# A bias table's trip through memory moved behind the first weight loads, and block sums built by one addition instead of sixteen

## The chip, the core and the metric

One core of one Trainium2 chip runs the whole program. The metric is the device time in microseconds of one execution, as the median over runs. TensorE does the matmuls, VectorE (DVE), ScalarE (ACT) and GpSimd (POOL) the element work, and SyncE (SP) issues the loads and stores on one queue, in order.

## What is computed

A sequence of 256 tokens of width 1024 goes through two blocks. The first block is a pool mixer beside an 8-head causal attention with a relative-position bias, then a gated MLP with a short convolution (width 2816) and a gated embedding. The second block has two layers: a native sparse attention (NSA) and a mixture of experts (MoE), then a latent attention (MLA) and again an MoE. Each MoE has 16 experts, of which two are chosen for a token. All arithmetic is float32.

Cut to what the change touches, the reference is

```python
# first block: bias of the attention logits, by bucket of the distance
bias_own = rel_bias.T[:, rel_bucket(t[:, None] - key_pos)]       # 8 heads
l_own = (q @ k.T) * scale + bias_own

# second block, NSA, compressed branch (for k and for v)
blk = t[:, tok_idx] + pe[None, None, :, None, :]   # 15 windows of 32 tokens, stride 16
blk = blk.transpose(0, 1, 3, 2, 4).reshape(B, 15, 4, 32 * 64)
k_cmp = silu(blk @ w1) @ w2
```

## The kernel before, in words

The weights don't fit on the chip; they are streamed from memory once, in chunks of 512 KB or 1 MB. Each f32 operand is split into a high and a low part, and a product is the sum of three matmuls on parts (`hilo`, `put_split`), so nearly all of TensorE's time is in matmuls of 128x128 weights on 256 or 512 columns.

No instruction is issued where it is written. The class `Plan` records each operation with its cost, its operands and, where two engines can do it, both alternatives (`record`, L324). Then `order` (L398) makes the program's order: time after time it takes the operation that can start first on some engine, by ranks among those that can start at nearly the same time, gives it its place in one arena of SBUF and one of 8 PSUM banks, and keeps a modelled time per engine. `emit` (L641) issues all of it, so in the profile nearly every instruction has line L649. Four things in it matter here:

- A load starts no earlier than `QUEUE` (L160) microseconds before the modelled time at which the DMA wire is free (L555). That sets how many loads stand in SP's queue ahead of the data.
- Where the planner sees a gap of more than `GAP` on TensorE, it puts in dummy matmuls of a zero tile `busy` (128x128 on 512 columns, bf16, L984), which keep the engine's clock up. Their number is fixed when the program is built.
- Tiles in the arena come free when the last reader is done, so a load that needs a place waits for that reader on SP, and all loads behind it wait too.
- A test that may run spare code when an expert has more tokens than slots (`overflow`, the `If` at L1836 and L1837) involves all engines; it has the name `ALL` in `record` and a modelled cost.

The bias table: `relative_bias` loads the 32x8 table and a 33x384 matrix of buckets, multiplies them on TensorE (8x384), copies the result to SBUF (`tab`), writes it to memory (`scr`), and reads it back with a step of one element per partition into `rev` (128x8x256, 1 MB read). `turned` turns it with four matmuls into the bias by token. `block1` (L1086) calls `relative_bias` first of all, then loads `xT` and the first 256 columns of `w_in` in four pieces each, then the next chunk `w1`, and calls `turned` after the load of `x`.

The compressed branch (`compressed`, L1360) runs once for k and once for v. It computes 256 feature columns into `kc` (128x2x256; head kv sits in one half of the partitions), and makes `kp`, in which each partition half holds the even or the odd tokens: 4 heads by 2 parities, 8 copies of 64x128. Then for each of the 16 positions j it adds a column of `pe` to a window of `kp` with step 8 (128x60, 4 heads by 15 windows) and writes it to `bt`; `bt` is the stationary operand of the 16 matmuls with `cmp_w1`.

Of the kernel before, what the change touches and what calls it, by code (L numbers as in the profile page):

```python
# [16 lines left out]
OP = mybir.AluOpType  # L17
# [132 lines left out]
class Plan:  # L150
# [6 lines left out]
    NEAR = 0.08  # L157
    LOOK = 80
    AHEAD = 16
    QUEUE = 3.0  # L160
    GAP = 0.6
    FIN = 0.0
    TICK = 10.24 / 3
# [157 lines left out]
        n = a[0].free_size()  # L321
        return n / 2400.0 * (2 if op == "transpose" or a[2].dtype == F32 else 1)

    def record(self, alts, reads=None, writes=None, name="ALL", cost=2.0, fn=None):  # L324
        if fn is None:
            _, op, a, k = alts[0]
            writes = [a[0]] + ([k["accum_out"]] if "accum_out" in k else [])
            reads = [x for x in list(a[1:]) + [v for n, v in k.items() if n != "accum_out"] if isinstance(x, bass.AP)]
# [69 lines left out]
    def order(self):  # L398
# [137 lines left out]
        for _ in range(n):  # L536
            best = None
            for e in engines:
                picks, low = [], None
                f = max(free.values()) if e == "ALL" else free[e]  # L540
                for _, _, o in cand[e][:self.AHEAD if e == "SP" else self.LOOK]:
# [12 lines left out]
                    if o.bytes:  # L554
                        s = max(s, wire - self.QUEUE)  # L555
                    if e == "ACT" and self.table(o) not in (None, table):
# [101 lines left out]
class K:  # L658
# [368 lines left out]
    def relative_bias(self):  # L1027

        nc, A = self.nc, self.A
        relb = self.stay([33, 8], "relb")  # L1030
        nc.vector.memset(relb, 1.0)
        nc.sync.dma_start(relb[:32], A["rel_bias"])
        bk = self.mid([384])
        nc.sync.dma_start(bk[:33], A["buckets"])
        p = self.ps()
        nc.tensor.matmul(p[:8, :384], relb, bk[:33], start=True, stop=True)
        tab = self.mid([384])
        nc.vector.tensor_copy(tab[:8], p[:8, :384])
        scr = self.scratch([8, 384], "scr")
        nc.sync.dma_start(scr, tab[:8])  # L1040
        rev = self.big([8, S])
        nc.sync.dma_start(rev, bass.AP(tensor=scr.tensor, offset=scr.offset, ap=[[1, 128], [384, 8], [1, S]]))
        return rev
# [42 lines left out]
    def block1(self):  # L1086
        nc, A = self.nc, self.A
        W = A["w_in"]
        rev = self.relative_bias()
        xT, w0 = self.big([8, S]), self.big([8, 256])  # L1090
        xTs = A["xT"].rearrange("(k p) t -> p k t", p=128)
        w0s = W[:, 512:768].rearrange("(k p) f -> p k f", p=128)
# [6 lines left out]
        for k in range(8):  # L1099
            g = self.v("g_mix_pre", k)  # L1100
            self.scaled(h[0][:, k], xT[:, k], g)
            nc.vector.scalar_tensor_tensor(h[1][:, k], xT[:, k], g, h[0][:, k], op0=OP.mult, op1=OP.subtract)
        w1 = self.chunk(W, 0, D, 1024, 256)
        self.setup2()
        self.routers()
        nc.sync.dma_start(x, A["x"].rearrange("(t p) d -> p t d", p=128))
        bias = self.turned(rev)
        r_tok = []
        for t in range(2):
            ss, dump = self.tiny(), self.mid([D])  # L1110
# [4 lines left out]
        v = self.mid([2, 512])  # L1115
# [244 lines left out]
    def compressed(self, W, h):  # L1360

        nc, A = self.nc, self.A

        blk, w1 = [], []
        for i, c0 in ((0, 768), (1, 1024)):
            kc, kp = self.mid([2, S]), self.mid([4, 128])
            self.feat(W, c0, 256, h, lambda j, p: self.copy(kc[:, j], p))
            for kv in range(4):
                src = kc[64 * (kv % 2):64 * (kv % 2) + 64, kv // 2].rearrange("p (m b) -> p b m", b=2)
                for b in range(2):  # L1370
                    self.copy(kp[64 * b:64 * b + 64, kv], src[:, b])
            bt = self.mid([16, 64])
            nc.gpsimd.memset(bt[:, :, 60:], 0.0)
            pe = self.v("pe")[:, 16 * i:16 * i + 16]
            for j in range(16):
                self.tscal(bt[:, j, :60].rearrange("p (k n) -> p k n", k=4), kp[:, :, j:j + 113:8], pe[:, j:j + 1], OP.add)
            blk.append(bt)
            w1.append(self.chunk(A["cmp_w1"][i], 0, 2048, 0, 128))
        p = self.ps()
# [7 lines left out]
        p = self.ps()  # L1387
# [6 lines left out]
        p = self.ps()  # L1394
# [12 lines left out]
        for c in range(2):  # L1407
# [5 lines left out]
            p = self.ps()  # L1413
# [630 lines left out]
```

## Time and profile before

| | us |
|---|---|
| median of three runs | 1055.67 |
| the three runs | 1057.70, 1055.67, 1055.63 |
| the profiled execution, its own time | 1057.48 |
| its span on the core | 1055.8 |
| TensorE busy in the span | 1025.5 (97%) |
| VectorE busy | 602.3 (57%) |
| ScalarE busy | 427.8 (41%) |

The span runs from the first to the last instruction of the profiled execution; 1.7 us of its time lie outside. Busy times of a stage are read from tables by stretches of the span, since the share over the span is a mean of stages with different limits. TensorE's busy time includes the dummy matmuls. In the rows, PE is TensorE, PEld its weight load, PEq its instruction queue, `span` a tile of the arena, `ps` a PSUM bank, `x3` a count of instructions.

### The profile page before, as it was taken

What the parts mean: (1) busy time and instruction counts of PE and PEld (TensorE: products, weight loads), DVE (VectorE), ACT (ScalarE), POOL (GpSimd) and SP (SyncE); (2) the same over time, 40 slices, a digit from 0 to 9 for tenths busy, and PEclk for the clock granted to TensorE, in tenths of its full rate; (3) what the DMA queues carried; (4) which work ended last, traced back from release to release, by engine and by line L of the source; (5) the groups of instructions that cost most, each with busy time, mean ns of one, the idle gap of its engine ahead of it and who ended that gap; (6) DMA issues with size and microseconds to landing.
All of it is one profiled execution on the core that took longest, in us unless ns stands there. A gap on an engine that the chain in (4) does not pass through costs nothing. (4 is left out here: it accounts for less than half of the span.)

```text
span 1055.8 us, 16466 instructions
## 1 busy us (share of the span) xinstructions
PE 1025.5 (97%) x6162; PEld 693.9 (66%) x6162; DVE 602.3 (57%) x1574; ACT 427.8 (41%) x984; POOL 13.8 (1%) x25
## 2 busy tenths in 40 slices
PE   9999999999999999999999899999999999999995
PEld 5887999999988888777434343435887534343432
DVE  5889996988766898995241111107996524010104
ACT  3567653554335556774231111106664413111113
POOL 0000000000000000100000000001000000000000
PEclk9999999999999999999999899999999999999998
DMA  8987546265595542288799999999768699999994
GB/s 275 365 258 247 172 157 217 82 205 175 197 307 160 180 160 81 82 303 315 268 373 387 382 345 387 385 381 375 285 213 309 219 375 386 386 386 387 387 384 157
DMA packets 172358, 292.84 MB, mean 277 GB/s; under 512 B 9251, under 2 KB 59340, under 8 KB 172268
## 3 DMA queue, kind: packets, MB, share of 16 engines
q1 hardware_dynamic: 172268, 291.69, 78.2%
q8 instruction: 51, 0.84, 0.3%
q14 instruction: 39, 0.32, 0.1%
HBM read 290.60 MB, written 1.06 MB: 276 GB/s over the span
## 5 line engine op out<-in xcount | busy, mean ns | idle before, releaser
L649 PE MATMUL ps<-span,span 128*128 128x256 f32 (+4 forms) x5432 | 940.2, 396 | 5.4 <-DVE span L649 3.8
L649 PEld LDWEIGHTS ps<-span,span 128*128 128x128 f32 (+1 forms) x5432 | 621.1, 173 | 292.9 <-issue 233.8
L649 DVE TENSOR_TENSOR span<-span,span 128x512 fp32r<-128x512 f32 (+7 forms) x464 | 275.0, 632 | 17.9 <-ACT span L649 13.1
L649 ACT CAST span<-span 128x512 fp32r<-128x512 f32 (+6 forms) x336 | 180.1, 581 | 44.0 <-DVE span L649 19.1
L649 DVE TENSOR_TENSOR span<-ps,span 128x512 fp32r<-128x512 f32 (+3 forms) x104 | 56.6, 549 | 144.1 <-ACT span L649 105.4
L649 DVE SCALAR_TENSOR_TENSOR span<-span,tiny,ps 128x512 f32<-128x512 f32 x16 | 12.0, 747 | 193.3 <-PE ps L649 181.8
L649 ACT CAST span<-ps 128x512 fp32r<-128x512 f32 (+1 forms) x65 | 33.1, 511 | 160.5 <-PE ps L649 156.5
L649 ACT COPY span<-ps 128x512 f32<-128x512 f32 (+3 forms) x105 | 50.2, 494 | 83.3 <-PE ps L649 72.4
L649 PE MATMUL ps<-cst,span 128*128 128x128 f32 (+1 forms) x363 | 59.5, 282 | 8.2 <-PEq L1837 3.2
L649 ACT ACTIVATE span<-ps 128x512 f32<-128x512 f32 (+3 forms) x33 | 18.5, 560 | 115.8 <-PE ps L649 110.1
L649 PEld LDWEIGHTS ps<-cst,span 128*128 128x128 f32 (+1 forms) x363 | 40.5, 142 | 24.4 <-issue 8.5
L649 ACT ACTIVATE span<-ps,vecs 128x256 f32<-128x256 f32 (+2 forms) x59 | 28.3, 512 | 68.1 <-PE ps L649 67.8
L649 ACT ACTIVATE span<-ps,tiny 128x256 f32<-128x256 f32 (+3 forms) x96 | 44.6, 472 | 19.8 <-DVE tiny L649 15.0
L649 ACT ACTIVATE span<-span 128x256 f32<-128x256 f32 (+4 forms) x36 | 16.1, 450 | 77.5 <-DVE span L649 76.8
L649 ACT ACTIVATE span<-span,tiny 128x256 f32<-128x256 f32 (+3 forms) x60 | 31.2, 535 | 15.6 <-DVE tiny L649 13.0
L984 PE MATMUL ps<-busy 128*128 128x512 bf16 x131 | 35.9, 423 | 1.1 <-POOL busy L980 1.1
L649 DVE TENSOR_REDUCE tiny<-ps 64x1 f32<-64x2 f32 (+3 forms) x78 | 30.0, 391 | 9.7 <-PE ps L649 7.4
L649 DVE CAST span<-span 128x512 fp32r<-128x512 f32 (+6 forms) x83 | 31.2, 382 | 3.7 <-DMA span<-in_w_in_dram 2.6
L649 DVE TENSOR_SCALAR span<-ps,vecs 128x256 f32<-128x256 f32 (+2 forms) x28 | 14.1, 512 | 30.2 <-ACT span L649 30.0
L649 DVE SCALAR_TENSOR_TENSOR span<-span,vecs,span 128x255 f32<-128x255 f32 (+2 forms) x52 | 24.3, 479 | 0.7
L984 PEld LDWEIGHTS <-busy 128*128 128x128 bf16 x131 | 13.3, 108 | 16.9 <-issue 6.5
L649 DVE TENSOR_SCALAR span<-span,tiny 128x256 f32<-128x256 f32 (+2 forms) x78 | 23.3, 325 | 0.1
(107 smaller groups left out, 342.1 us busy)
## 6 DMA issues: line engine op xcount, KB each, us to landing
span<-in_moe_w_gate_dram SPq DMA_DIRECT2D x128, 512.0 KB, 7.9
span<-in_moe_w_up_dram SPq DMA_DIRECT2D x128, 512.0 KB, 7.6
span<-in_moe_w_down_dram SPq DMA_DIRECT2D x128, 512.0 KB, 7.4
span<-in_w_up_dram SPq DMA_DIRECT2D x22, 1024.0 KB, 5.4
span<-in_w_out_dram SPq DMA_DIRECT2D x12, 1024.0 KB, 10.4
span<-in_w_down_dram SPq DMA_DIRECT2D x11, 1024.0 KB, 7.2
span<-in_w_in_dram SPq DMA_DIRECT2D x7, 1024.0 KB, 12.9
span<-in_nsa_w_in_dram SPq DMA_DIRECT2D x7, 1024.0 KB, 8.4
```

Source lines behind the costliest of these rows:

```text
L649: getattr(eng, op)(*[real(x) for x in a], **{n: real(x) for n, x in k.items()})
L984: return lambda: nc.nc.tensor.matmul(nc.banks[bank], busy, busy.unsqueeze(1).to_broadcast([128, 4, 128]), start=True, stop=True)
```

## The change

Four edits. `QUEUE` goes from 3 to 8. The modelled cost of an operation of name `ALL` goes from 2.0 to 3.2; it issues nothing. `relative_bias` is cut in two: the loads, the matmul and the copy (`relative_bias`) are now written behind the loads of `xT`, `w0` and `w1`, and the write and read of `scr` (`shifted`) behind the load of `x`. In `compressed` the 8 copies become 4 of two heads each, and the 16 additions one, over a window whose three steps (head, window, position) overlap in memory, with `pe` broadcast over heads and windows.

```diff
-    QUEUE = 3.0
+    QUEUE = 8.0
...
-    def record(self, alts, reads=None, writes=None, name="ALL", cost=2.0, fn=None):
+    def record(self, alts, reads=None, writes=None, name="ALL", cost=3.2, fn=None):
...
         tab = self.mid([384])
         nc.vector.tensor_copy(tab[:8], p[:8, :384])
+        return tab
+
+    def shifted(self, tab):
+        nc = self.nc
         scr = self.scratch([8, 384], "scr")
         nc.sync.dma_start(scr, tab[:8])
         rev = self.big([8, S])
...
     def block1(self):
         nc, A = self.nc, self.A
         W = A["w_in"]
-        rev = self.relative_bias()
         xT, w0 = self.big([8, S]), self.big([8, 256])
...
         w1 = self.chunk(W, 0, D, 1024, 256)
+        tab = self.relative_bias()
         self.setup2()
         self.routers()
         nc.sync.dma_start(x, A["x"].rearrange("(t p) d -> p t d", p=128))
-        bias = self.turned(rev)
+        bias = self.turned(self.shifted(tab))
...
             self.feat(W, c0, 256, h, lambda j, p: self.copy(kc[:, j], p))
-            for kv in range(4):
-                src = kc[64 * (kv % 2):64 * (kv % 2) + 64, kv // 2].rearrange("p (m b) -> p b m", b=2)
+            for v in range(2):
+                src = kc[self.halves(v)].rearrange("p k (m b) -> p b k m", b=2)
                 for b in range(2):
-                    self.copy(kp[64 * b:64 * b + 64, kv], src[:, b])
+                    self.copy(kp[self.halves(b)].rearrange("p (k v) m -> p v k m", v=2)[:, v], src[:, b])
             bt = self.mid([16, 64])
             nc.gpsimd.memset(bt[:, :, 60:], 0.0)
-            pe = self.v("pe")[:, 16 * i:16 * i + 16]
-            for j in range(16):
-                self.tscal(bt[:, j, :60].rearrange("p (k n) -> p k n", k=4), kp[:, :, j:j + 113:8], pe[:, j:j + 1], OP.add)
+
+            pe = self.v("pe")[:, 16 * i:16 * i + 16].unsqueeze(1).unsqueeze(1).to_broadcast([128, 4, 15, 16])
+            win = bass.AP(tensor=kp.tensor, offset=kp.offset, ap=[kp.ap[0], [128, 4], [8, 15], [1, 16]])
+            self.tt(bt[:, :, :60].rearrange("p j (k n) -> p k n j", k=4), win, pe, OP.add)
```

What the planner makes of it moves more than these lines. The order of the real matmuls' work stays the same in number and shape; the dummies go from 131 to 114. Before the first MoE's test there are 83 before and 79 after, and between the two tests 48 and 35. By place: 12 and 25 around the table's matmul become one run of 37; 4 become 3 early in the first attention; in the compressed branch's layer 15, 2 and 5 become 9 and 3; at the entry of the first MoE 4 and 4 become 10 and 5; in the MLA layer 17, 7, 2 and 7 become 18 and 9; at the entry of the second MoE 10 and 5 become 4 and 4.

SP's queue at the start of the program (names are arena tiles and inputs; `scr` is the table in memory). Before:

```order
L649 DMA vecs<-in_vecs_dram 128x16
L649 DMA relb<-in_rel_bias_dram 32x8
L649 DMA span_115<-in_buckets_dram 33x384
L649 DMA span_117<-in_xT_dram 128x2x256
L649 DMA span_119<-in_w_in_dram 128x2x256
...
L649 DMA scr<-span_115 8x384
...
L649 DMA span_150<-in_w_in_dram 128x8x256
L649 DMA span_200<-scr 128x8x256
L649 DMA cst<-in_cblob_dram 128x343
```

The same place now:

```order
L649 DMA vecs<-in_vecs_dram 128x16
L649 DMA span_112<-in_xT_dram 128x2x256
L649 DMA span_116<-in_w_in_dram 128x2x256
...
L649 DMA span_124<-in_w_in_dram 128x8x256
L649 DMA relb<-in_rel_bias_dram 32x8
L649 DMA span_133<-in_buckets_dram 33x384
L649 DMA cst<-in_cblob_dram 128x343
...
L649 DMA scr<-span_133 8x384
...
L649 DMA span_204<-scr 128x8x256
L649 DMA span_227<-in_w_out_dram 128x4x512
```

Table and buckets are now 11th and 12th in the queue instead of 2nd and 3rd; the write of `scr` goes from 9th to 21st, its read from 14th to 26th, behind all of the first block's chunks of `w_in` and ahead of `w_out`.

VectorE in the compressed branch (`span_3951` and `span_4032` before, `span_2626` now, are `kp`; `span_105` and `span_109` are `bt` for k and v). Before:

```order
L649 COPY span_3948<-ps_73 128x256
L649 TENSOR_TENSOR span_3958<-span_150,span_3958 128x512
L649 COPY span_3951<-span_3948 64x128 x3
L649 TENSOR_SCALAR span_105<-span_3951,vecs 128x60 x16
L649 RECIPROCAL tiny<-tiny 128x2
L649 CAST span_1320<-span_403 128x512
L649 TENSOR_TENSOR tiny<-tiny,gates 128x2
L649 TENSOR_TENSOR span_1320<-span_403,span_1320 128x512
L649 COPY span_4032<-span_3948 64x128 x2
L649 COPY span_4074<-ps_71 128x2x128
L649 TENSOR_SCALAR span_109<-span_4032,vecs 128x60 x16
```

The same place now:

```order
L649 COPY span_2626<-span_772 64x2x128 x3
L649 TENSOR_TENSOR span_3955<-span_3289,span_3955 128x512
L649 TENSOR_TENSOR span_105<-span_2626,vecs 128x60x16
L649 CAST span_246<-span_116 128x512
L649 TENSOR_TENSOR span_246<-span_116,span_246 128x512
L649 COPY span_2626<-span_772 64x2x128 x3
L649 TENSOR_REDUCE tiny<-ps_69 128x2
L649 TENSOR_TENSOR span_109<-span_2626,vecs 128x60x16
```

Two runs of 16 additions became two single ones. VectorE does 6 of the copies in both orders (before 4 for k, one of them ahead of these rows, and 2 for v; now 3 and 3, each with twice the elements), ScalarE 10 before and 2 now.

## Rows read from the trace of the kernel before

**Rows 1.** Part 1 of the page: busy time, share and instructions of each engine.

```profile
PE 1025.5 (97%) x6162; PEld 693.9 (66%) x6162; DVE 602.3 (57%) x1574; ACT 427.8 (41%) x984; POOL 13.8 (1%) x25
```

**Rows 2.** Waits of TensorE: releaser, us in total, times, longest us.

```profile
PE ps L649 <- DVE span L649: 7.9, 19, 1.3
PE ps L649 <- PEq L1837: 3.2, 1, 3.2
```

**Rows 3.** Table by stages: length; busy PE, PEld, DVE, ACT, POOL; granted clock; DMA share; GB/s.

```profile
12.00:36.00 24.00, 22.78 (x141) 18.57 (x140) 18.81 (x61) 11.66 (x22) 0.00 (x0) 1.00 1.04 355
350.00:470.00 120.00, 114.67 (x947) 99.06 (x945) 113.47 (x395) 78.62 (x236) 2.88 (x6) 1.00 0.50 169
...
510.00:540.00 30.00, 30.00 (x138) 10.47 (x138) 6.73 (x13) 6.34 (x11) 0.95 (x1) 1.00 0.98 348
...
560.00:590.00 30.00, 30.00 (x140) 10.50 (x138) 2.44 (x5) 2.73 (x5) 0.00 (x0) 1.00 1.05 387
...
600.00:610.00 10.00, 8.69 (x34) 4.45 (x36) 0.85 (x2) 1.74 (x3) 0.00 (x0) 0.66 1.01 367
```

**Rows 4.** Timeline of TensorE, the start: start us, us, instruction, count.

```profile
6.19 0.81 PE L649 MATMUL ps<-span,relb 33*8 33x384 f32 x2
6.93 5.57 PE L984 MATMUL ps<-busy 128*128 128x512 bf16 x25
12.15 6.37 PE L649 MATMUL ps<-span,span 128*128 128x256 f32 x50
```

**Rows 5.** Timeline of SP, the start.

```profile
4.20 0.47 SPq L649 DMA_DIRECT2D span<-in_xT_dram  x1
7.61 0.30 SPq L649 DMA_DIRECT2D scr<-span  x1
```

**Rows 6.** VectorE's groups in 350 to 470 us, by shape: count, busy us, mean ns.

```profile
L649 DVE TENSOR_TENSOR span<-span,span 128x512 fp32r<-128x512 f32 x41 | 27.5, 685 | 0.2
...
L649 DVE TENSOR_SCALAR span<-span,tiny 128x256 f32<-128x256 f32 x23 | 7.3, 347 | 0.0
L649 DVE TENSOR_SCALAR span<-span,vecs 128x60 f32<-128x60 f32 x32 | 6.1, 273 | 0.1
...
L649 DVE TENSOR_TENSOR span<-span,span 128x256 f32<-128x256 f32 x10 | 4.2, 418 | 0.2
L649 DVE TENSOR_SCALAR span<-span,tiny 128x128 f32<-128x128 f32 x17 | 4.2, 279 | 0.0
...
L649 DVE COPY span<-span 64x128 f32<-64x128 f32 x6 | 1.3, 223 | 0.5 <-ACT span L649 0.4
```

**Rows 7.** ScalarE's copies in 350 to 470 us, same columns.

```profile
L649 ACT COPY span<-span 64x128 f32<-64x128 f32 x10 | 3.1, 305 | 0.3
```

**Rows 8.** Timeline of all engines in 384 to 392 us.

```profile
385.57 3.07 DVE L649 TENSOR_SCALAR span<-span,vecs 128x60 f32<-128x60 f32 x16
...
389.59 0.62 PE L649 MATMUL ps<-cst,span 128*128 128x128 f32 x2 [1.69 <-ACT span L649]
```

**Rows 9.** Table by stages, of the dummy matmuls (tile `busy`) alone.

```profile
350.00:470.00 120.00, 5.25 (x22) 2.05 (x22) 0.00 (x0) 1.00 0.50 169
490.00:500.00 10.00, 2.89 (x8) 0.83 (x8) 0.00 (x0) 0.87 0.74 269
720.00:755.00 35.00, 7.80 (x33) 3.08 (x33) 0.00 (x0) 0.95 1.02 364
820.00:828.00 8.00, 5.10 (x15) 1.89 (x15) 0.00 (x0) 0.79 0.15 57
```

**Rows 10.** Timeline of TensorE, the same stretch of both MoE layers.

```profile
575.33 22.82 PE L649 MATMUL ps<-span,span 128*64 128x512 f32 x104
...
613.39 1.09 PE L649 MATMUL ps<-span,identr 128*128 128x512 f32 x4
...
902.30 22.82 PE L649 MATMUL ps<-span,span 128*64 128x512 f32 x104
...
935.97 1.09 PE L649 MATMUL ps<-span,identr 128*128 128x512 f32 x4
```

## The prediction

> **What bounds the kernel now.** I read the busy times first: TensorE is busy for 97% of the span, no other engine for more than 57% [rows 1]. Then the waits of TensorE: it waits 7.9 us in all for VectorE's tiles, 3.2 us once for its own sequencer, and there is no line on which it waits for a DMA [rows 2]. So TensorE sets the time, and a change can move it in four ways: its real work, its waits, its clock, or the dummy matmuls on the zero tile `busy` that the planner puts into gaps it foresees. The order of instructions says that the real matmuls are the same in number and shape. It has 131 dummies before and 114 after. What is left is to look, place by place, at whether the gap under a dummy or a wait closes.
>
> The table by stages shows where gaps can close [rows 3]. Between 350 and 470 us (the second block's first attention, in which the compressed branch lies) VectorE is busy for 113.47 of 120 us: there it runs beside TensorE at its limit, and TensorE idles for 120 - 114.67 = 5.3 us. In the MoE stretches TensorE has no gap and the weights stream at 348 to 387 GB/s.
>
> **The parts, with their sums** (against the profiled execution, 1057.48 us; it is 1.81 us above the median of the three runs, so each end is moved by that at the end).
>
> *Start (A).* Before, 12 dummies run, then the bias table's matmul at 6.19 us, then 25 dummies until 12.15 us, where real work begins without a wait [rows 4]. A dummy at full clock costs (12.15 - 6.93) / 25 = 0.21 us. The table matmul takes 6.93 - 6.19 = 0.74 us; after, the same 37 dummies stand in one run with no matmul between them, so real work can begin up to 0.74 us earlier, if its data is there. It should be: three DMA issues (two loads and the write of `scr`) leave the head of SP's queue, and with the write goes the hole in which SP stood still for its data, from 4.20 + 0.47 to 7.61, 2.94 us [rows 5]. The matmul comes back later on the path, so the net of this is 0. In 12 to 36 us TensorE idles 24 - 22.78 = 1.22 us [rows 3]; the chunks that feed it are now issued earlier, and I take half of it, -0.6. One dummy less in that stretch (4 before, 3 after) adds -0.2: **A = -0.8**. Bounds: -2.0 (the 0.74 of the table matmul and all of the 1.22 gone) and +2.9 (the `scr` trip now stands behind most of the `w_in` chunks, and its wait, as long as today's hole, falls on the `turned` matmuls). I stay far from the upper end because the trip is issued while those chunks' matmuls still lie ahead of TensorE.
>
> *Compressed branch (B).* VectorE loses 32 additions of 128x60, 6.1 us in all, and gets two of 128x960 [rows 6]. The trace has no TENSOR_TENSOR of 960 elements: 256 take 418 ns and 512 take 685, which is 1.04 ns for each more, so 960 should take 685 + 448 x 1.04 = 1.15 us, 2.3 us for both (an estimate; this addition writes with a stride, which no row has; twice as long, 4.6 us, is my upper bound). The six copies that VectorE did (223 ns each, 1.3 us) stay six in the new order but have 256 elements; the nearest row of that size from the arena is 347 ns: +0.8. VectorE is relieved of 6.1 - 2.3 - 0.8 = 3.0 us. ScalarE's 10 copies of 305 ns become 2 of twice the size: about -2.3 us there [rows 7], which is not the limit. What is freed on VectorE in a stretch where it is busy 95% I count one for one. A second reading agrees: behind the run of 16 additions (3.07 us) TensorE waits 1.69 us [rows 8], and the dummies of the stretch go from 22 to 12, 10 x 0.21 = 2.1 us; 3.8 us of gap is there to take the 3.0. **B = -3.0.** Bounds: 0 (the planner's order turns other VectorE work into the wait) and -7 (idle 5.3 plus 2.1 of dummies).
>
> [...] The rows show that VectorE's one-source additions and multiplications cost (347 - 279) / 128 = 0.53 ns per element and its two-source ones 1.04 [rows 6]: the new instruction streams at half the rate. [...] By that rate alone 1920 elements would cost 2.0 us instead of 1.0, and B would be +1.0 and no gain. But 128x60 costs 273 ns where 60 x 0.53 is 32: nearly all of an old addition is its fixed part, and 30 of 32 fixed parts go. The row decides.
>
> *MLA (C).* Between the two branches the order has 35 dummies in place of 48. In 720 to 755 us there are 33 of them [rows 9], where now 18 + 9 stand and none later in that layer. The change has no instruction of its own here; the deeper queue lets loads be issued earlier, and the last 7 dummies, which stand ahead of a matmul that waits for a load, go. 6 x 0.21 gives **C = -1.3**; bounds 0 (a wait takes the dummies' place) and -3.5 (half of the 7.80 us of dummies less a rest).
>
> *MoE entries (D).* The first has 15 dummies now in place of 8, the second 8 in place of 15; 8 took 2.89 us and 15 took 5.10 [rows 9], so +2.2 and -2.2: **D = 0**, bounds -1 and +1.
>
> *Depth of the queue in the MoE layers (E).* QUEUE from 3 to 8 lets a load be planned up to 8 us before the wire is free. The stream ran at 348 GB/s in 510 to 540 us against 387 later, 30 x (1 - 348/387) = 3.0 us lost, but TensorE was busy in all 30 us [rows 3], and no wait on a load is listed [rows 2]. What hides it is the lead that the stream has on TensorE; were that gone, 3.0 us per layer would show. **E = 0**, bounds -2 and +2.
>
> *The overflow test's cost* (2.0 to 3.2) changes a number of the planner and no instruction: 0 by itself.
>
> Sum: -0.8 - 3.0 - 1.3 = **-5.1 us**: 1052.4 for a run like the profiled one, 1055.67 - 5.1 = **1050.6** for the median.
>
> **Rivals.**
>
> *R1, the second branch stalls as the first does.* [...] The same stretch of program took 613.39 - 575.33 = 38.06 us there and 935.97 - 902.30 = 33.67 us in the second layer [rows 10]: the stall costs 4.4 us, and only one of two branches pays. Whether one pays must hang on where it lies in the program, and both lie elsewhere now (4 dummies with their weight loads fewer ahead of the first, 17 ahead of the second). If the second pays too: -5.1 + 4.4 = -0.7, 1055.0. For it: one of two paid before. Against: the second did not, with the same instructions around it. [...]
>
> *R2, the first branch no longer stalls.* Up to -4.4 more; but the weight stream is full there (387 GB/s), and a TensorE that comes earlier meets it sooner; I count little more than half, 2.5: 1048.1. For and against as in R1.
>
> *R3, only the places change.* VectorE's freed time is given back because its order around the additions is another (the long addition stands in front of small operations that release TensorE, 1.15 us at once instead of in pieces of 0.19), and waits come where dummies stood: between -1 and +1, 1055.7. For it: the planner makes the order of the whole program anew, not of these lines alone. Against: VectorE's sum in that stretch falls for certain.
>
> *R4, the deep queue blocks (the other side).* SP issues in order. A load planned 8 us early whose buffer comes free late holds all loads behind it. Today's hole is 3.0 us per MoE layer; if it becomes three times as long and the stream's lead is used up, each layer loses 6 us more: -5.1 + 12 = +6.9, 1062.6. It decides for slower from (5.1 + 2.1) / 2 = 3.6 us per layer on. For it: the lead is what hides it, and no row gives it at the end of a layer. Against: no TensorE wait on a load anywhere [rows 2].
>
> **How the numbers follow.** A measurement of this kernel can tell 0.2%, 2.1 us, from no change. Forecast 0.55, R1 0.13, R2 0.12, R3 0.11, R4 0.09. Faster: the forecast, R2, and the fifth of R1 in which the parts gain more: 0.70. Same: most of R1, and R3: 0.21. Slower: R4, 0.09. The range takes in the forecast with B near its lower bound and R2 (1050.6 - 5.6, 1045) up to R3 with its +1 (1056.7): 1045 to 1056.7. R4 and the far bounds stay outside.
>
> **What would show it.** A: real work at about 11.4 us, the `turned` matmuls without a wait. B: two additions of 1.1 to 1.2 us, VectorE's busy time between the first attention's ends down by 3 us, no 1.7 us wait. C: no dummies behind the MLA layer's first 30 us. R1, R2: the sequencer's wait twice, or not at all. R4: a wait of TensorE on a `moe_w` load. I am wrong if TensorE's waits for VectorE stay near 7.9 us, or if additions of 960 take over 2 us.

## The result, and the profile after

The changed kernel takes 1045.27 us (median of four runs, 1043.71 to 1045.87) against 1055.65 for the kernel before: ratio 0.9898, 95% interval [0.9878, 0.9919]. It is faster, as forecast, by 10.4 us where the forecast was 5.1, and 0.3 us above the lower end of the range. The profiled execution took 1043.71 us, its span is 1042.0.

The waits of TensorE after the change (releaser, us in total, times, longest):

```profile
PE ps L649 <- PEq L1842: 3.1, 1, 3.1
PE ps L649 <- DVE span L649: 2.2, 5, 1.2
PE ps L649 <- ACT span L649: 2.0, 6, 0.7
PE ps L649 <- DVE selb L649: 1.3, 1, 1.3
PE ps L649 <- DVE tiny L649: 1.2, 2, 0.8
PE ps L649 <- DMA span<-in_moe_w_gate_dram: 1.1, 2, 0.9
```

The wait for VectorE's tiles falls from 7.9 to 2.2 us, that for the sequencer stays [rows 2], and a wait on a load appears that was not there. In a second trace of each kernel (`before_again`, `after_again`, below) it is 7.0 and 4.1 us for VectorE's tiles, and 0.6 us on loads after the change.

The table by stages (columns as in [rows 3]):

```profile
12.00:36.00 24.00, 24.00 (x151) 20.99 (x150) 21.30 (x66) 12.96 (x24) 0.00 (x0) 1.00 1.08 362
350.00:466.00 116.00, 111.92 (x927) 97.55 (x926) 110.34 (x364) 76.99 (x231) 2.18 (x6) 1.00 0.55 184
502.00:532.00 30.00, 30.00 (x139) 10.62 (x140) 6.71 (x13) 6.73 (x11) 0.95 (x1) 1.00 1.05 382
592.00:602.00 10.00, 8.28 (x44) 3.61 (x44) 1.24 (x2) 1.74 (x3) 0.96 (x1) 1.00 1.05 385
```

At the start TensorE has no gap left in 24 us. VectorE is as full in the second block's first attention as it was (110.34 of 116 us, 95%). Behind the first test the granted clock is 1.00, where it was 0.66 [rows 3]; that belongs to this execution, since in `after_again` it is 0.83 in the same stretch.

The timeline of TensorE, the start:

```profile
1.13 10.13 PE L984 MATMUL ps<-busy 128*128 128x512 bf16 x37 [1.13 <-POOL busy L980]
10.91 3.21 PE L649 MATMUL ps<-span,span 128*128 128x256 f32 x24
13.97 0.82 PE L984 MATMUL ps<-busy 128*128 128x512 bf16 x3
14.44 1.78 PE L649 MATMUL ps<-span,span 128*128 128x256 f32 x12
16.15 0.81 PE L649 MATMUL ps<-span,relb 33*8 33x384 f32 x2
```

Real work begins at 10.91 instead of 12.15 us [rows 4].

VectorE's new additions and copies in 346 to 466 us (count, busy us, mean ns), then the dummies alone by stages:

```profile
L649 DVE TENSOR_TENSOR span<-span,vecs 128x960 f32<-128x960 f32 x2 | 3.7, 1870 | 0.0
...
L649 DVE COPY span<-span 64x256 f32<-64x256 f32 x6 | 1.7, 287 | 0.1
```

```profile
350.00:466.00 116.00, 2.93 (x12) 1.09 (x12) 0.00 (x0) 1.00 0.55 184
484.00:493.00 9.00, 3.56 (x15) 1.40 (x15) 0.00 (x0) 1.00 0.21 61
705.00:740.00 35.00, 6.17 (x27) 2.57 (x27) 0.00 (x0) 0.95 1.06 380
```

An addition takes 1.87 us, not 1.15. The dummies take 2.93 us in the compressed branch's layer (5.25 before) and 6.17 in the latent attention's (7.80) [rows 9]; the 15 at the first MoE's entry take 3.56.

To see where the time came from I set TensorE's real matmuls of the traces against each other: both kernels stream the same 2,054,412 columns, so the time at which each has streamed the same share can be compared, whatever the order. The second trace of each kernel is taken in, since single executions differ by some us. Times are in us, the last column is the mean of after less the mean of before for that stage alone:

| up to (rounded share of the columns) | before, twice | after, twice | stage |
|---|---|---|---|
| first block's MLP (34%) | 348.7, 349.4 | 346.2, 345.6 | -3.2 |
| into the first MoE (49%) | 525.1, 524.6 | 517.6, 518.3 | -3.8 |
| behind the first test (58.5%) | 619.1, 617.6 | 609.0, 611.2 | -1.3 |
| first MoE's last pairs (68%) | 705.7, 704.3 | 695.6, 697.8 | -0.1 |
| into the second MoE (79%) | 848.6, 846.1 | 834.5, 834.2 | -4.7 |
| its last pairs (94%) | 990.2, 987.8 | 975.0, 976.0 | -0.5 |
| last matmul | 1043.8, 1041.2 | 1029.8, 1029.8 | +0.8 |

The traces of the two kernels are 12.7 us apart in the mean, the medians 10.4: both traces of after are about 1.6 us under its median. The table says where, not to the last us how much.

### The profile page after: what moved, and what is told of

Read it like the earlier page. It is cut to its first block, busy times and chain, and to the rows that moved or that the text cites. A ratio compares the mean times of both kernels' runs of the same rounds, so it can differ in the third digit from the quotient of the medians.

```text
span 1042.0 us, 16440 instructions
## 1 busy us (share of the span) xinstructions
PE 1016.8 (98%) x6145; PEld 692.2 (66%) x6145; DVE 597.2 (57%) x1535; ACT 425.2 (41%) x985; POOL 12.2 (1%) x25
## 5 line engine op out<-in xcount | busy, mean ns | idle before, releaser
L649 PE MATMUL ps<-span,span 128*128 128x256 f32 (+5 forms) x5432 | 938.4, 396 | 3.5 <-DVE span L649 1.2
L649 PEld LDWEIGHTS ps<-span,span 128*128 128x128 f32 (+2 forms) x5432 | 621.9, 173 | 291.2 <-issue 229.4
L649 DVE TENSOR_TENSOR span<-ps,span 128x512 fp32r<-128x512 f32 (+3 forms) x104 | 56.6, 549 | 144.1 <-ACT span L649 113.4
L649 ACT COPY span<-ps 128x512 f32<-128x512 f32 (+4 forms) x112 | 52.8, 489 | 94.7 <-PE ps L649 85.8
L649 ACT ACTIVATE span<-ps,tiny 128x256 f32<-128x256 f32 (+3 forms) x96 | 44.5, 473 | 16.9 <-DVE tiny L649 12.3
L984 PE MATMUL ps<-busy 128*128 128x512 bf16 x114 | 29.4, 407 | 1.1 <-POOL busy L980 1.1
```

The lines of the kernel that those rows point to most:

```text
L649: getattr(eng, op)(*[real(x) for x in a], **{n: real(x) for n, x in k.items()})
L984: return lambda: nc.nc.tensor.matmul(nc.banks[bank], busy, busy.unsqueeze(1).to_broadcast([128, 4, 128]), start=True, stop=True)
```

## The experiments

Ratios below are to the kernel before, run beside each group of kernels, with 95% intervals. Beside the different groups the kernel before had medians of 1055.65 to 1056.9 us, so a difference of 1 to 2 us between kernels of different groups shows nothing.

**Each edit alone.** Three kernels, each the kernel before with one of the hunks above.

```diff
 only_sums:  the hunk in compressed(), nothing else
 only_bias:  the hunks in relative_bias() and block1(), nothing else
 only_queue: QUEUE = 3.0 -> 8.0, nothing else
```

> The kernel before with the compressed branch's new copies and additions alone; bias trip, queue depth and the overflow test's cost as before. Theory 1 (the forecast's: the parts add up, and what VectorE is relieved of in the compressed branch comes off TensorE's path one for one): the two additions measured 1.87 us each, so VectorE is relieved of 6.1 - 3.7 - 0.4 = 2.0 us and the time is about 1053.6. Theory 2 (the gain is in the order that the planner makes of all edits together; each edit alone gets other gaps): the order has 136 dummies, 5 more than before, 20 of them in this layer where there were 22: within 1 us of before, 1054.7 to 1056.7.

> The kernel before with the bias table's trip moved and nothing else. Theory 1: the start alone gains, 2.6 us by the changed kernel's trace (forecast 0.8), so 1053.0 to 1054.9. Theory 2: the new order also has 12 dummies in the first attention of the second block in place of 22, though nothing was edited there, and 41 in place of 33 in the latent attention's layer: 2.6 + 2.1 - 1.7 = 3.0 us less, 1052.6, and the gain shows in the second block's first layer as well.

> The kernel before with QUEUE at 8 and nothing else. Theory 1: little, -1.3 at most in the latent attention's layer: 1054.4. Theory 2: 139 dummies, 12 in place of 22 in the second block's first layer, 41 in place of 33 in the latent attention's layer: about -0.4, 1055.2, and the place of the gain is the second block's first layer, the place of the loss the latent attention's. Either way the transfers of the MoE layers take longer from issue to landing (10.7 us in place of 7.6) without TensorE waiting.

Measured: `only_sums` 1054.46 (0.9993 [0.997, 1.0015]), `only_bias` 1051.08 (0.9953 [0.9937, 0.997]), `only_queue` 1052.80 (0.9975 [0.9954, 0.9996]). By the totals theory 2 wins: the additions alone can't be told from no change. The other two are faster than either theory had them. By the traces theory 2 does not win: in `only_sums` TensorE gains 2.1 us from the end of the first block to the first MoE's entry (143.7 us in place of 145.8 in both traces of before), about what theory 1 gives, and loses 2.6 us or more at the first test and 1.4 at the second. There its timeline shows the longest wait of all runs:

```profile
593.40 0.60 PE L649 MATMUL ps<-cst,span 128*128 128x128 f32 x4
600.28 11.33 PE L649 MATMUL ps<-span,span 128*128 128x256 f32 x44 [6.28 <-PEq L1838]
611.45 1.09 PE L649 MATMUL ps<-span,identr 128*128 128x512 f32 x4
```

In `only_bias` the first test costs 0.6 us and the second, free in the changed kernel, 2.46 us and then 10.73 us (granted clock 0.72 in 920 to 926 us) for 44 matmuls that take 9.35 at the first test of the changed kernel's trace, at a granted 1.00. So the tests blur every comparison of complete kernels, and theory 3 (the tests' price) was formed.

**The additions in a fixed order.** `after_sixteen` keeps the changed kernel's order and issues each new addition as the 16 old ones.

```diff
-            self.tt(bt[:, :, :60].rearrange("p j (k n) -> p k n j", k=4), win, pe, OP.add)
+            o = nc.vector.tensor_tensor(bt[:, :, :60].rearrange("p j (k n) -> p k n j", k=4), win, pe, op=OP.add)
+            o.alts = [(engine, cost, [the 16 tensor_scalar calls])]   # in short
```

> The changed kernel with every instruction in the place it has there, but each of the two additions of 960 elements issued as the 16 of 60 elements that it replaces (same plan, same dummies, same copies). Theory 1: VectorE gets 6.1 - 3.7 = 2.4 us back and TensorE loses as much: 1047.7. Theory 2: TensorE's order there has room for it: within 0.5 us of the changed kernel, 1045.3 to 1045.8.

1046.86 us (0.9919 [0.9893, 0.9944]), 1.6 over the changed kernel: on the side of theory 1, 0.8 short of it, but the two ratios' intervals overlap. The same comparison without the tests, next, is the cleaner one.

**Without the tests.** `emit` in `overflow` returns at once, so the two tests and the spare code behind them are left out; the order of all else is as it was. Beside the two kernels, `before_one_notest` (the kernel before with each run of 16 additions issued as one) and `after_sixteen_notest`.

```diff
         def emit():
+            return
             og_, x_, hd_, hT_, xT_, oge_, b_ = (plan.real(a) for a in (og, x, hd, hT, xT, oge, bank))
```

> The kernel before in its own order, with both overflow tests and the spare code behind them left out (no expert overflows with these inputs, so the code is never entered). Theory 3 (part of the difference is what the two tests cost TensorE: a stall that is another length in every program, and the lower clock behind it): the stretch around the test is 17.75 us where nothing stalls; here it took 23.9 and 18.9, so 6.2 + 1.1 = 7.3 us go and the profiled execution would be 1050.2, the median 1048.4 to 1051. Theories 1 and 2, by which the tests play no part in the difference: before less its waits at the tests, 3.7 us, 1052.

> The changed kernel in its own order, without the overflow tests and the spare code. Theory 3: its stretches around the tests took 21.4 and 17.75 us, so 3.7 us go: 1041.6; the difference to the kernel before without tests is then 7 to 8 us instead of 10.4. Theories 1 and 2 (no part of the gain is in the tests): 10.4 us under the kernel before without tests. A fourth reading, that the weight stream already bounds the end of the changed kernel (0.9 us of wait on a load at 993 us): less than 2 us of the 3.7 come out, 1043.5 or more.

> The kernel before without the overflow tests, in its own order, with each run of 16 additions issued as one addition of 960 elements at the place of the first (copies and all else as before). Theory 1: VectorE is relieved of 6.1 - 3.7 = 2.4 us and TensorE gains that or more (3.5 us in the trace with the edit alone): 2.4 to 3.5 us under the kernel before without tests. Theory 2: within 0.5 us of it.

> The changed kernel without the overflow tests, in its own order, with the 16 additions in place of the one. Theory 1: 2.4 us over the changed kernel without tests, up to 4.5 by the traces (that much more was lost in the compressed branch's layer). Theory 2: within 0.5 us of it. If the weight stream bounds the end, part of the loss is swallowed: 1 to 2 us.

Measured: 1052.55 (0.9964 [0.9952, 0.9976]), 1044.06 (0.9883 [0.9858, 0.9908]), 1050.60 (0.9946 [0.9929, 0.9962]) and 1046.17 us (0.9903 [0.9878, 0.9928]). The additions give 1.95 us in the order of before and 2.1 in that of after, each known to about 1 us: **for the additions theory 1 holds, with 2.0 us for 2.4 us of VectorE's time**. Where it is lost with sixteen can be read from TensorE's timeline of `after_sixteen_notest`, right behind the second run of additions:

```profile
392.35 0.67 PE L649 MATMUL ps<-cst,span 128*128 128x128 f32 x4 [1.57 <-DVE span L649]
393.20 0.41 PE L649 MATMUL ps<-cst,span 128*128 128x128 f32 x2 [0.18 <-DVE span L649]
395.41 0.76 PE L649 MATMUL ps<-cst,span 128*128 128x128 f32 x5 [1.10 <-ACT span L649]
```

The same matmuls wait 0.28 us in all in `after_notest`. Leaving the tests out gives before 4.0 us, the figure of theories 1 and 2 (3.7) and not theory 3's 7.3, and after some 1.2, not 3.7. The difference is then 8.5 us where theory 3 had 7 to 8 and the others 10.4. Up to 2 us of the 10.4 may so be the tests', but the totals don't show it: the interval of the 10.4 reaches from 8.6 to 12.9 us. That after gained 1.2 and not 3.7 fits the fourth reading (a bound at the end).

**Two edits of three, and one, without tests.** Made from the hunks above, with `emit` cut short as before. `no_queue_notest` and `no_bias_notest` are the changed kernel with one edit taken back, so they keep the number 3.2; `only_bias_notest` has 2.0.

> The kernel before with the bias trip moved and nothing else, without overflow tests and spare code. By the traces the start gains 2.6 to 3.5 us, against 0.8 in the forecast. If the start is all that the move gives: 1049 to 1050 (the kernel before without tests is 1052.55). If the remade order of the second block's first layer gains as well (1.8 us in the trace of the same edit with tests): 1047 to 1048.5. If the 4.9 us of the edit with tests came from the tests: 1051 or more.

> The changed kernel with QUEUE back at 3 (the planner makes the order anew), without tests and spare code. If the depth of the queue gives nothing (forecast: 1.3 at most): 1044 to 1045.4, as the changed kernel without tests (1044.06). If it is what gains 4 us in the latent attention's layer: 1046 to 1048, with 41 dummies there in place of 27, and TensorE without a wait on loads at the ends of the MoE layers.

> The changed kernel with the bias trip at the start again, without tests and spare code. Parts that add up: 2.0 us for the additions and 2.6 for the queue under the kernel before without tests: 1048. If the moved trip gives only the forecast's 0.8: 1044.9.

1045.75 (0.9896 [0.9846, 0.9946]), 1047.10 (0.9899 [0.9868, 0.993]) and 1045.42 us (0.9896 [0.9867, 0.9926]). Of the 8.5 us the moved trip alone gives 6.8, more than any reading had for it; the additions and the queue without it give 7.1, where adding the parts gave 4.6. `no_queue_notest` falls in its second range, with the 41 dummies in the latent attention's layer that belong to it, but not without a wait on loads (2.8 us). All three kernels have 12 dummies in the compressed branch's layer; this is the row of `only_bias_notest`, which still has its 32 additions:

```profile
350.00:466.00 116.00, 2.93 (x12) 1.09 (x12) 0.00 (x0) 1.00 0.50 170
```

So **the ten dummies less don't come from the additions**. From the end of the first block to the first MoE's entry TensorE takes 146.2 us in `before_notest`, 144.1 in `only_bias_notest` and 142.2 in `after_notest`: some 2 us for the order and some 2 for the additions. And the totals of the parts don't add up: what is gained ahead of an MoE layer is not all kept behind it.

**Is it the weight stream that takes it?** Three trials. `after_notest_more` issues eight of the first MoE's entry dummies three times.

```diff
                 if callable(call):
                     call()
+                    if it is one of the 65th to 72nd dummies: call() twice more   # in short
```

> The changed kernel without tests and spare code, and 16 more dummies (3.4 us at full clock) at the entry of the first MoE layer, all other instructions in their places. If the weight stream bounds the ends of the MoE layers (TensorE waits 4.0 us for loads in the kernel without them): within 1 us of 1044.06, and those waits fall by about 3 us. If TensorE is the bound there: 1047.5.

Its median is 1047.67 (1045.10 to 1050.48; 0.992 [0.9896, 0.9944]), which is what the reading with TensorE as the bound had, and its waits on loads fall by 0.4 us only, to 3.6. Its trace speaks for the stream: it is as long as that of `after_notest` (1045.10 against 1044.90). But that sets the fastest of its eight executions beside the slowest of the other's five. So this trial doesn't show the stream as the bound; it speaks rather against it.

```diff
-                    ws_ = [self.chunk(A[w_][l, 2 * pr + e], 128 * k, 256, 0, 512) for e in range(2)]
+                    if pr != 1 or not gu:
+                        ws_ = [self.chunk(A[w_][l, 2 * pr + e], 128 * k, 256, 0, 512) for e in range(2)]
+                        held = [ws_] if k == 0 else held + [ws_]
+                    else:
+                        ws_ = held[k // 2]
```

> The changed kernel without tests and spare code, in which the second pair of experts of each MoE layer uses its gate weights in place of its up weights: 8 loads of 512 KB (10.8 us of the stream at 387 GB/s) fewer in each layer, no matmul fewer; it computes something else there. If the weight stream bounds the last pairs of both layers: no wait on a load at the last pair (2.1 and 1.9 us now, and the lower clock behind each), 4 to 8 us less than 1044.06, so 1036 to 1040. If TensorE is the bound there: 1043 to 1045.

1041.63 us (0.987 [0.9835, 0.9906]): 2.4 under `after_notest`, short of either expectation. The 8 loads saved in each layer were not saved time: the stream, which runs at 379 to 387 GB/s in 500 to 560 us of `after_notest`, ran at 340, 325 and 320 GB/s in the three 20 us stretches there. TensorE still waited at the first layer's last pair (1.03 and 0.22 us), but the clock stayed at 1.00 there.

The third is `no_cost_notest`, the same order up to that place with the planner's number at 2.0:

```diff
-    def record(self, alts, reads=None, writes=None, name="ALL", cost=3.2, fn=None):
+    def record(self, alts, reads=None, writes=None, name="ALL", cost=2.0, fn=None):
```

> The changed kernel without tests and spare code, planned with the modelled cost of 2.0 instead of 3.2 for the operation that is left out: the only thing that differs is the order that the planner makes behind the first test's place. If that number is worth nothing (the forecast's 0): 1044.06 within 1 us. If the gain in the latent attention's layer hangs on it: its dummies are 17, 2 more, 7 and 7 at the places of before, and 2 to 4 us of lead are lost there; up to that much in the time, less what the weight stream gives back: 1045 to 1047.

1042.34 us (0.9875 [0.9838, 0.9911]), outside both expectations; that it is faster than `after_notest` is not shown, since the intervals overlap nearly whole. TensorE's timeline at the last pair of the first MoE, `after_notest`:

```profile
670.19 0.64 PE L649 MATMUL ps<-cst,span 128*128 128x128 f32 x4
672.97 26.08 PE L649 MATMUL ps<-span,span 128*64 128x512 f32 x104 [2.14 <-DMA span<-in_moe_w_gate_dram]
698.88 0.62 PE L649 MATMUL ps<-cst,span 128*128 128x128 f32 x4
```

and `no_cost_notest`, which came there 1.24 us later in this execution:

```profile
671.43 0.64 PE L649 MATMUL ps<-cst,span 128*128 128x128 f32 x4
671.83 25.77 PE L649 MATMUL ps<-span,span 128*128 128x512 f32 x110
697.44 0.60 PE L649 MATMUL ps<-cst,span 128*128 128x128 f32 x4
```

The earlier one waits 2.14 us, then runs 104 matmuls in 26.08 us that take 23.59 at the same place in the changed kernel's trace, where the granted clock is 1.00 (674 to 698 us). It leaves these rows 1.44 us later with six matmuls fewer done; where both have streamed 68% of the columns it is 3.4 us behind. The clock in between, table by stages of `after_notest`:

```profile
674.00:682.00 8.00, 8.00 (x32) 3.23 (x33) 0.50 (x1) 0.58 (x1) 0.00 (x0) 0.83 1.05 387
```

In both kernels the stream runs at 387 GB/s through that stretch. So TensorE meets the stream at the ends of the layers in these traces, and the wait there cost more than its length (2.14 us, and 2.5 more in the 104 matmuls); how much of the total the stream takes stays open. From there to the second MoE's entry `no_cost_notest` loses 3.9 us to `after_notest`, 3.1 of them ahead of the latent attention, at the end of the MoE layer, and 0.8 in the latent attention's layer, where it has 33 dummies, as before.

**The number 3.2 in the complete kernel.**

> The changed kernel, complete, planned with the modelled cost of 2.0 for the overflow test instead of 3.2. Without the tests this order was 1.7 us under the changed kernel's, since TensorE came 1.25 us later to the last pair of the first MoE layer and had no wait and no lower clock there, though it lost 3.5 us in the latent attention's layer. If that carries over: 1043 to 1044. If it hung on the missing tests: the 3.5 us lost show, and it is 1045.3 to 1048.8.

1045.65 us (0.9894 [0.9874, 0.9914]), not to be told from the changed kernel (1045.27). Its trace has no wait on a load, so a gain ahead of the second MoE that it lacks may be what the changed kernel gives back there; that is not shown. No complete kernel was found that beats the changed one.

**The form of the addition.**

```diff
-            win = bass.AP(tensor=kp.tensor, offset=kp.offset, ap=[kp.ap[0], [128, 4], [8, 15], [1, 16]])
-            self.tt(bt[:, :, :60].rearrange("p j (k n) -> p k n j", k=4), win, pe, OP.add)
...
+            pe = self.v("pe")[:, 16 * i:16 * i + 16].unsqueeze(2).unsqueeze(3).to_broadcast([128, 16, 4, 15])
+            win = bass.AP(tensor=kp.tensor, offset=kp.offset, ap=[kp.ap[0], [1, 16], [128, 4], [8, 15]])
+            self.tt(bt[:, :, :60].rearrange("p j (k n) -> p j k n", k=4), win, pe, OP.add)
```

> The changed kernel in its own order, in which the addition of 960 elements runs with the position outermost: it reads with step 8, as the 16 additions did, and writes runs of 60 elements that lie together, instead of reading 16 together and writing each with a step of 64 elements. If the step of the writes is what makes it 1.87 us instead of the 1.15 worked out from the rows: 1.1 to 1.3 us each, VectorE is relieved of 1.4 us more, and the time is up to 1.4 us under the changed kernel, 1044 to 1045. If the form as such is slow: 1.8 to 1.9 us each, 1045.3.

```profile
L649 DVE TENSOR_TENSOR span<-span,vecs 128x960 f32<-128x960 f32 x2 | 3.9, 1958 | 0.0
```

1.96 us each, 1045.89 us (0.9912 [0.9878, 0.9946]): to take the step away from the writes doesn't make it faster. But one operand steps at every element in both forms, the writes by 64 in the one and the reads by 8 in the other, so whether a step on either side is what costs stays open; a form without one was not tried.

**Second traces.**

> The kernel before, unchanged, for a second trace. If the price of a test belongs to the order of the program: again about 23.9 and 18.9 us for the stretches around the two tests, with a wait of 3.2 us and the lower clock behind it in the first. If it belongs to the execution: another pair of values, such as 21.4 us for a wait of 3.1 us at full clock, and a span that differs by as much.

> The changed kernel, unchanged, for a second trace. If the price of a test belongs to the order: again 21.4 and 17.8 us around the tests and a wait of about 1 us for loads at the end of the second MoE layer. If it belongs to the execution: other values, up to 2.5 us more where the lower clock follows the wait. The dummies' places, the two additions (1.87 us) and the latent attention's layer must be as in its first trace.

1054.93 and 1043.68 us, one execution each. The first test, timeline of `before_again`:

```profile
574.80 22.82 PE L649 MATMUL ps<-span,span 128*64 128x512 f32 x104
...
600.81 0.89 PE L649 MATMUL ps<-cst,span 128*128 128x128 f32 x4 [3.18 <-PEq L1837]
601.35 10.73 PE L649 MATMUL ps<-span,span 128*128 128x256 f32 x44
611.91 1.09 PE L649 MATMUL ps<-span,identr 128*128 128x512 f32 x4
```

and of the changed kernel, first trace:

```profile
567.79 22.82 PE L649 MATMUL ps<-span,span 128*64 128x512 f32 x104
...
593.72 0.63 PE L649 MATMUL ps<-cst,span 128*128 128x128 f32 x4 [3.11 <-PEq L1842]
...
603.29 1.10 PE L649 MATMUL ps<-span,identr 128*128 128x512 f32 x4
...
888.25 22.82 PE L649 MATMUL ps<-span,span 128*64 128x512 f32 x104
...
920.78 1.09 PE L649 MATMUL ps<-span,identr 128*128 128x512 f32 x4
```

From the 104 matmuls to the `identr` ones it is 38.06 [rows 10] and 37.11 us in before's two traces, 35.50 and 37.04 in after's (605.51 - 568.47): in both orders the wait is 3.1 to 3.2 us each time, and whether the lower clock follows is the execution's. (`after_turned`, in the order of after, takes 38.07 us there.) So the cheap first test in after's first trace was luck of that execution. For the second test it is 33.67 and 33.78 against 32.53 and 32.54: the 1.2 us are the order's.

## Why the prediction had the sign right and the size wrong

The table of columns and the timelines of the four traces give what each place gained, against its term of the sum (us, mean of the two traces of each kernel; B ends and C begins and ends at the first dummy of the run there):

| place | forecast | measured |
|---|---|---|
| start to the end of the first block (A) | -0.8 | -3.2 |
| from there to the first MoE's entry (B) | -3.0 | -3.6 |
| the two MoE entries (D) | 0 | -1.0 |
| around the two tests | 0 | -2.5 |
| end of the first MoE layer, behind 68% | 0 | -2.2 |
| latent attention's layer, to the second MoE's entry (C) | -1.3 | -1.7 |
| all else, the second MoE's last pairs (E) among it | 0 | +1.5 |
| sum | -5.1 | -12.7 |

B and C come out near their forecasts. **The steps that failed are the reading "In the MoE stretches TensorE has no gap", by which the MoE layers got no term but a D and an E of 0, and the size of A.** The first was read from stretches of 30 us well ahead of the layer's end. In its place the runs show 2.2 us at the end of the first MoE layer and 2.5 around the tests (of which the 1.3 at the first go with the clock of the single executions); for A they show 3.2 instead of 0.8. Why the end of the layer got shorter stays open: from the 68% mark to the first dummy behind the layer it is 16.9 us in before, 14.7 in after, 14.6 in `only_queue`, 14.7 in `only_sums` and 17.7 in `only_bias`, so it goes with the order that the planner makes and with no one edit.

**A, the start: -0.8, measured -3.2.** The direction was right. Two steps were too small. I let the table matmul's 0.74 us return on the path for a net of 0, but real work begins 1.24 us earlier (12.67 and 10.39 us, so 2.28, in the second traces) and the matmul fills time without a new gap. And I took half of the 1.22 us of gaps in 12 to 36 us, three waits for VectorE of about 0.4 us each; all of them went. `only_queue` has a start as good (2.2 us in its trace) with the table's loads still first: there the read of `scr` moves back behind the constants, `x` and two more chunks. Common to both is that this 1 MB read no longer stands ahead of the chunks, and also that SP's hole ahead of the write of `scr` [rows 5] no longer holds up loads of `w_in` and `xT`. Neither was tried by itself, so which of them is the cause stays open.

**B, the compressed branch: -3.0, measured -3.6 in the traces (-3.8 in the table of columns, whose line takes in the MoE's entry), of which 2.0 are the additions.** The mechanism was right, and TensorE's gain per VectorE time nearly so (2.0 for 2.4). The 1.69 us wait of [rows 8] was VectorE's in the end: ScalarE, which released TensorE, had itself waited for a small operation that stood behind the 16 additions.

```profile
389.14 0.69 ACT L649 ACTIVATE span<-span,tiny 128x128 f32<-128x128 f32 x2 [2.77 <-DVE tiny L649]
```

The addition was mis-sized: 1.87 us against my 1.15, inside my bound of 2.3. The copies were priced high (287 ns, not 347). A step that failed here is "a second reading agrees": I took the ten dummies less as another view of the same 3.0 us. They are a second gain, 5.25 - 2.93 = 2.3 us, and come with the new order even where nothing was edited in that layer (144.1 us in `only_bias_notest` for 146.2, above). Both together less the waits that came (0.46 and 0.70 us and smaller ones, on ScalarE) make about the 3.6. That the sum came out near the forecast is so in part luck.

**C, the latent attention: -1.3, measured -1.7 in its own layer.** The dummies there take 6.17 us instead of 7.80. The number is near, but by luck: the mechanism I gave (the deeper queue ends the dummies ahead of a load) isn't it, since `only_queue`, with that queue alone, has 41 dummies there in place of before's 33. It is the order of all edits together that has 27. The line in the table of columns has -4.7, because it takes in the second MoE's entry and the end of the first MoE layer. There, ahead of C's dummies, three waits stand in before's trace:

```profile
710.27 0.66 PE L649 MATMUL ps<-cst,span 128*128 128x128 f32 x4 [0.26 <-DVE span L649]
711.60 8.36 PE L649 MATMUL ps<-span,span 128*64 128x512 f32 x36 [0.67 <-ACT span L649]
720.26 0.96 PE L649 MATMUL ps<-span,picks 128*128 128x512 f32 x3 [0.30 <-DVE span L649]
```

They are gone after. The step **"changes a number of the planner and no instruction: 0 by itself"** failed too: a planner's number moves the order of all that follows, and with 2.0 the latent attention's dummies are 33 again and 3.9 us are lost up to the second MoE (`no_cost_notest`, above). In the complete kernel no such loss shows in the time (`no_cost`).

**D = 0, measured -1.8 in the first pair of traces and -0.3 in the second.** I let 8 dummies cost 2.89 us and 15 cost 5.10 [rows 9] at either entry. Timeline of TensorE, first entry after, in `after`:

```profile
488.72 2.32 PE L984 MATMUL ps<-busy 128*128 128x512 bf16 x10
491.04 0.27 PE L649 MATMUL ps<-selb,bfs 128*128 128x16 bf16 x5
491.17 1.24 PE L984 MATMUL ps<-busy 128*128 128x512 bf16 x5
492.20 5.16 PE L649 MATMUL ps<-span,span 128*128 128x256 f32 x32
```

and in `after_again`:

```profile
488.18 3.85 PE L984 MATMUL ps<-busy 128*128 128x512 bf16 x10
...
492.00 1.33 PE L984 MATMUL ps<-busy 128*128 128x512 bf16 x5
```

The same ten dummies take 2.32 us at a granted 1.00 (488 to 491 us) and 3.85 us at a granted 0.60 (488 to 492 us). From the first dummy to the next real group it is 3.48 us (492.20 - 488.72) and 4.80 in the two traces of after, where it was 4.07 and 3.77 before; at the second entry it is 3.57 and 3.48 for 4.74 and 4.85. So the price of a dummy at an entry goes with the clock, which at the first entry is the execution's; the rows that I priced the dummies from had a granted 0.87 and 0.79 [rows 9]. That the dummies keep the clock up is not shown: here ten in a row ran at the 0.60. One trace of each kernel was too little to size this term.

**E = 0** and the sentence that no wait on a load is listed held for before alone. After, TensorE is 13 us earlier at the last pair of the second MoE and meets the stream: 1.1 us of wait, and +0.8 us in the last line of the table of columns. R4's place was right and its cause is not needed: `no_queue_notest`, with QUEUE at 3, has 2.8 us of such waits.

**R1 and R2**, on the 3.2 us wait at the first test [rows 2] and the granted 0.66 behind it [rows 3], were not what happened there, since the wait stayed (3.1 to 3.2 us in the four traces), but their subject mattered: in the traces the stretches around the tests got 1.3 and 1.2 us shorter, the second in both executions. The price differs from program to program: a wait of 3.1 to 6.3 us or 0.6 at the first test, none to 2.95 at the second (`only_queue`), with the same instructions around it. No run here shows why.

## What to carry to other kernels

Where a planner makes the order, an edit's own gain can be the smaller part, here 2.0 of 8.5 us for the additions: price the edit in a fixed order, and the new order apart, dummy by dummy and wait by wait, since they add up rather than confirm each other. Look for gaps at the ends of a stage too, not only in its middle, and take a second trace before a term is sized by a stretch at the lower clock. Before gains are added, look for the stage that has the least slack to a second resource: here the end of each MoE layer, where TensorE came to wait for the weight stream once it was earlier. Leave a blurring part (a test, a branch) out of both kernels when the totals of single edits and their traces disagree.

## Not expected of the hardware

A wait of TensorE cost more than its length: in `after_notest` 2.14 us on a load were followed by a granted clock of 0.83 over 8 us, and 104 matmuls took 2.5 us longer; a wait of 1.03 us in `after_notest_light` had no such tail (granted 1.00). The same 3.1 us wait at the first test was followed by a granted 1.00 in one execution of the changed kernel and 0.83 in the other (592 to 602 us), 1.5 us apart. At the first MoE's entry ten matmuls of the zero tile, in one order, took 2.32 us in one execution and 3.85 in the other (granted 1.00 and 0.60).
